# Two weight sums of the up projection formed by DRAM copies and adding transfers instead of on VectorE

## The chip, the cores and the metric

The kernel runs on one core of one Trainium2 chip. The metric is the device time of one execution in microseconds (us). A second execution was recorded by the hardware profiler; its page and trace are what this document reads. Engines are named as the profile names them: PE is TensorE (PEld its weight loads), DVE is VectorE, ACT is ScalarE, POOL is GpSimd, and SP is SyncE, which here only starts transfers.

## The reference

One layer of a decoder trunk, at 1024 positions and width 1024, all in float32:

```
h = rmsnorm(x)
[q | k | v | u | s | gate_a | gate_b] = h @ w_in
branch A: sliding-window attention (window 128, 8 query heads, 2 key heads)
branch B: u * (tril(W_s) @ rmsnorm(gelu(s)) + b), in chunks of 128 positions
x = x + (sigmoid(gate_a) * (A @ w_oa) + sigmoid(gate_b) * (B @ w_ob)) @ w_out
z = rmsnorm(x) @ w_up                       # 1024 x 5632
zc = causal depthwise convolution of z, width 3, plus bias
x = x + (silu(zc[gate half]) * zc[value half]) @ w_down
```

What the change touches is the product with w_up and the way the gates' and the down projection's inputs are combined for the same scheme.

## The kernel before

Matrices are held transposed: features on the 128 partitions, positions along the free dimension. Every float32 operand of a product is split in a high part (rounded to the form that PE takes) and a low part (the rest), and each product is three matmuls, high by high, high by low and low by high. ACT makes the high parts (`copy_hi`, L87), POOL or DVE the low ones by a subtraction (L988 for the weights of the gates and the up projection).

The gates, the up and the down projection are computed by a fast scheme on 2 x 2 blocks with seven products in place of eight (Strassen's scheme in Winograd's form). For the up projection, a *pair* is a gate tile and a value tile of 128 output features each. The four blocks of its weights are called A11, A12 (one tile's first and second half of the input features) and A21, A22 (the other tile's). Four sums of them are needed besides: S1 = A21 + A22, S2 = S1 - A11, S3 = A11 - A21 and S4 = A12 - S2. The right-hand blocks B11 to B22 have sums T1 to T4 of their own. `Blocks.prod` (L1028) runs one of the seven products, 12 matmuls of 512 columns; `Blocks.sums`, `fast_pair`, `gate_pair` and `v_end` add the products up on DVE. There are 22 pairs for the up projection and 8 for the gates.

S1 and S3 of the 22 up pairs are formed ahead of the up stage. `sums_load` loads A11 of a pair (256 KB) and A21 and A22 (512 KB) from w_up, `sums_step` makes the two sums on DVE in SBUF (L620, tile `ls`) and stores them to DRAM (tile `sum`, 512 KB). This is done 12 times among the gate pairs, twice in each from the third on, and 10 times among the branch products, where `branch` calls it. In the up stage `Left.load_q` and `Left.load_s3` load S1 and S3 back, with A22 from w_up; POOL makes S2 and S4 from them (`sum_s2`, `sum_s4`).

The stages in time: projection of keys and values (to about 50 us), attention (to 180 us), the normed values and the spatial products of branch B (`v_phase`, to about 220 us), the gates (`v_end`, `gate_pair`, to 381 us), the branch and output products (`run_jobs`, to 571 us), the up stage with the convolution (`fast_pair`, to 978 us) and the down projection.

Attention is one loop over n from 0 to 19 (L649 and on). Iteration n computes the scores of block n (`s_mm`, `s_mask`), the softmax of block n-1 (`s_exp`, whose last step is on POOL, L480), transposes and splits block n-2 (`p_split`, with four selects on POOL, L502 and L504) and multiplies block n-4 by the values (`pv_mm`). PE's waiting time is filled with pieces of other projections (`filler`). `weights(n)` splits the weight tile due in that iteration (the low part on POOL, L108 or L191) and starts the load of a later one on SP. The next stage's `v_phase` runs over s from 0 to 7: PE makes the halves of the value tile s, ACT the GELU, `v_rsqrt(s)` on DVE and POOL (L128, L129) the scale, `v_norm(s)` on DVE the normed values (L755), which frees the PSUM tile, and `v_split` the two parts for the spatial products (`sgu_mm`).

The order of work is written by hand: within a region marked `manual_schedule()` each engine issues its instructions in the order of the code. Attention is one such region and `v_phase` to the end another; where instructions of one region fall among those of the other on the same engine is left to the planner. Transfers that SP starts stand in SP's queue in the same way, and one that waits for a buffer holds up those behind it. POOL starts no transfer in this kernel.

Of the kernel before, what the change touches and what calls it, by code (L numbers as in the profile page):

```python
# [41 lines left out]
def body(ctx, tc, nc, a):  # L42
# [216 lines left out]

    st = {}  # L260

    def q_proj(n):
# [356 lines left out]
    def sub(eng, out, x, y, op=ALU.subtract):  # L619
        eng.tensor_tensor(out, x, y, op=op)  # L620
        return out

    def x_gain(r, ks):
        for k in ks:
            x = xr_raw[r][:, k, :]
            nc.scalar.activation(x, x, AF.Copy, scale=cp[:, 186 + 4 * r + k:187 + 4 * r + k])

    def x_sums(ks, first):
        for k in ks:
            x0 = xr_raw[0][:, k, :]  # L630
            if first:
                sub(nc.vector, x0[:, L], x0[:, H], x0[:, L])
            else:
                x1 = xr_raw[1][:, k, :]
                sub(nc.vector, x0[:, H], x1[:, H], x0[:, H])
# [6 lines left out]
    for n in range(20):  # L642
        if n < 16:
            s_mm(n)
            s_mask(n)
        if 0 <= n - 1 < 16:
            s_exp(n - 1)
        if n < 16:
            s_max(n)  # L649
        if 0 <= n - 4 < 16:  # L650
            pv_mm(n - 4)
        q_new = filler(n, 0)
        if 0 <= n - 2 < 16:
# [12 lines left out]
        if n == 17:  # L666
            x_gain(0, (0, 1))
        if n == 18:
            x_gain(0, (2, 3))
            x_sums((0, 1), True)  # L670
        if n == 19:
            x_sums((2, 3), True)
        for t, p in u_done:
            nc.vector.tensor_tensor(uT[:, t, :], p, rstd_b, op=ALU.mult)
        u_done.clear()
        if n + 2 < 16:
            q_trans(n + 2)
            q_split(n + 2)
        for q in [3] + q_new if n == 0 else q_new:
            q_norm(q)  # L680
# [105 lines left out]
    def v_phase():  # L786
# [32 lines left out]
    def v_end():  # L819
# [52 lines left out]
        nx.load_q()  # L872
        sums_load()
        q.prod(q.v1, "S2", "T2")
# [9 lines left out]
        nc.scalar.copy(x5, e)  # L884
        nc.vector.tensor_tensor(x7, x7, e, op=ALU.add)
        nc.vector.tensor_tensor(q.g1, x5, q.g1, op=ALU.add)
        nc.vector.tensor_tensor(q.v1, x7, q.v1, op=ALU.add)
        nc.vector.tensor_tensor(q.v0, q.u2, q.v0, op=ALU.add)
        q.scale(q.zv)
# [38 lines left out]
    class Left:  # L928
# [28 lines left out]
        def sum_s3(self):  # L957
            self.s3 = s3_pool.tile([128, 4, 128], F, tag="s3", name=nm("s3"))
            sub(nc.gpsimd, self.s3, self.p[:, 0:4], self.q[:, 0:4])

        def sum_f3(self):

            sub(nc.gpsimd, self.p[:, 0:4], self.q[:, 4:8], self.r[:, 0:4])

# [14 lines left out]
        def sum_s2(self):  # L979
            self.r = raw("lr")  # L980
            sub(nc.gpsimd, self.r[:, 0:4], self.q[:, 0:4], self.p[:, 0:4])

        def sum_s4(self):
            sub(nc.gpsimd, self.r[:, 4:8], self.p[:, 4:8], self.r[:, 0:4])

# [25 lines left out]
    class Blocks:  # L1011
# [38 lines left out]
    sums = {"load": 0, "make": 0}  # L1050

    def sums_load():

        i = sums["load"]
        if i < NPAIR:
            x = pools["ls"].tile([128, 3, 4, 128], F, tag="ls", name=nm("ls"), bufs=2)
            nc.sync.dma_start(x[:, 0], a["wup"][2 * i][:, 0:4])
            nc.sync.dma_start(x[:, 1:3], a["wup"][2 * i + 1].rearrange("p (b k) m -> p b k m", b=2))
            sums[i] = x
            sums["load"] += 1  # L1060

    def sums_step():

        i = sums["make"]
        if i < NPAIR:
# [6 lines left out]
            pools.setdefault("sum", {})[i] = t  # L1072
            sums["make"] += 1


# [26 lines left out]
    def gate_pair(c, prev):  # L1102
# [93 lines left out]
    def branch(n):  # L1196
        br, c = B_ORDER[n]

        def main(w):
# [66 lines left out]
    def out_tile(i):  # L1266
        d = D_ORDER[i]

        def main(w):
# [20 lines left out]
            if d < 4:  # L1290
                eng = nc.gpsimd if i < 6 else nc.vector
                right_split("B11", k, h[:, L], eng)
                sub(nc.vector, h[:, L], h[:, H], h[:, L])
                right_split("T1", k, h[:, L], eng)
            else:
                g = hs_[k]
                sub(nc.vector, g[:, H], h[:, H], g[:, H])
# [3 lines left out]
                t2 = sub(nc.vector, pools["raw2"][:, k, :], h[:, H], g[:, L])  # L1301
                sub(nc.vector, pools["raw4"][:, k, :], h[:, L], t2)
            if i == 0:
# [6 lines left out]
    def last_tile(w, ac):  # L1310
# [27 lines left out]
        g = hs_[k]  # L1338
        sub(nc.vector, g[:, H], h[:, H], g[:, H])
        right_split("B22", k, h[:, H], nc.vector)  # L1340
        right_split("T3", k, g[:, H], nc.vector)
        t2 = sub(nc.vector, pools["raw2"][:, k, :], h[:, H], g[:, L])
        sub(nc.vector, pools["raw4"][:, k, :], h[:, L], t2)

# [98 lines left out]
    def first_pair():  # L1443
# [31 lines left out]
        nx.split_s3()  # L1475
        nc.vector.tensor_tensor(x7, x7, u2, op=ALU.add)
        q.prod(q.g1, "S4", "B22", more=True)
# [9 lines left out]
        q.u2 = u2  # L1487
        nc.vector.tensor_tensor(q.v1, u2, x7, op=ALU.add)
        nc.vector.tensor_tensor(q.v0, u2, q.v0, op=ALU.add)

# [9 lines left out]
    def fast_pair(n, prev, q, hooks, rms=None):  # L1500
# [41 lines left out]
        if nx and not rms:  # L1542
            nx.split_p()
        nc.vector.tensor_tensor(x7, x7, q.g1, op=ALU.add)
        if rms:
# [235 lines left out]
def layout(x, mix_norm, w_in, q_norm, k_norm, sinks, sgu_norm, w_s, b_s,  # L1781
# [17 lines left out]
    up_order = np.stack([np.arange(NPAIR), np.arange(NPAIR) + NPAIR], 1).reshape(-1)  # L1799
    wup = tiles(w_up, 8)[up_order]  # L1800

    def pcol(v):
# [20 lines left out]
        "wout": tiles(w_out, 8),  # L1823
        "wup": wup,
        "wdown": c(w_down.reshape(NPAIR, 128, 1024)),
# [20 lines left out]
```

## Time and profile before

| | |
|---|---|
| Median of 3 runs | 1193.23 us (1193.14 to 1193.96) |
| Profiled execution | 1193.8 us, span 1192.1 us |
| Granted PE clock | 1.000 over the span |
| HBM read, written | 139.63 MB, 50.59 MB |
| DVE, sums of S1 and S3 (L620, tile ls) | 44 instructions, 269.7 to 468.0 us |
| POOL, rsqrt of the normed values (L129) | 8 instructions in 180 to 222 us, idle before them 21.9 us |
| PE waits that end on POOL or DVE in attention | 11 groups, the longest of them 1.3 us in all |

The span reaches from the first to the last instruction; the execution's own time has some microseconds around it. A row of instructions names the line of the kernel, the engine, the operation, and the tiles as output<-inputs with their shapes; behind `x` stands how many there are. Brackets at the end of a row give how long the engine stood idle before it and which instruction ended that. `SPq` rows are transfers that SP started: the length is that of the issue, not of the transfer.

### The profile page before, as it was taken

To read this page: it belongs to the slowest core of one execution; us is meant where nothing else is said; L and a number is where in the kernel's file an instruction comes from. 1 tells how busy PE (TensorE), PEld (TensorE's weight loads), DVE (VectorE), ACT (ScalarE), POOL (GpSimd) and SP (SyncE) were. 2 spreads that over 40 slices of the span, in tenths; PEclk is the share of its full clock that TensorE was granted. 3 is DMA by queue.
4 is the path that set the end of the run, shared out by engine and by line. 5 is a ranking of instruction groups with operands and counts; after the bars stand their busy time and mean duration, and the time that the engine had idled before them with its cause. 6 is when DMAs were issued, how large, how long until landed. Compare 5 with 4: busy or idle time off the path is not lost.

```text
span 1192.1 us, 15888 instructions
## 1 busy us (share of the span) xinstructions
PE 1180.0 (99%) x5890; PEld 1000.9 (84%) x5890; DVE 877.8 (74%) x1028; ACT 541.8 (45%) x832; POOL 567.4 (48%) x364
## 2 busy tenths in 40 slices
PE   8999999999999999999999999999999999999998
PEld 8989989988888888888888888888888888888887
DVE  7798975745638565668897788878788798865674
ACT  8555567644335222234544444444444445434331
POOL 2367685487768222343756575656657551000000
PEclk9999999999999999999999999999999999999999
DMA  7110133037786997342143342423333258966471
GB/s 272 35 54 19 54 136 130 5 130 260 245 315 212 347 327 278 125 165 100 54 142 108 104 143 98 148 91 124 108 131 124 89 209 290 373 230 194 151 233 67
DMA packets 79134, 191.27 MB, mean 160 GB/s; under 512 B 8913, under 2 KB 9169, under 8 KB 79057
## 3 DMA queue, kind: packets, MB, share of 16 engines
q1 hardware_dynamic: 79056, 190.26, 45.9%
q8 instruction: 46, 0.75, 0.3%
q14 instruction: 32, 0.25, 0.1%
HBM read 139.63 MB, written 50.59 MB: 160 GB/s over the span
## 4 chain that ended last, share of the span: by engine, by line
PE 89%; DVE 4%; POOL 1%; issue 1%; ACT 0%; POOLq 0%; DVEq 0%; ACTq 0%
PE pz L1028 48%; PE pd L1672 10%; PE pdy L1672 8%; PE px L93 2%; PE px L92 2%; PE po L93 2%; PE po L92 2%; PE po L91 2%; PE px L91 2%; PE pvs L91 1%; PE pvs L92 1%; PE pvs L93 1%; DVE ya L529 1%; PE pq L91 1%; PE pq L93 1%; PE pq L92 1%
## 5 line engine op out<-in xcount | busy, mean ns | idle before, releaser
L1028 PE MATMUL pz<-T,qh 128*128 128x512 f32 x472 | 145.6, 390 | 0.0
L988 POOL TENSOR_TENSOR pl<-lp,ph 128x1024 fp32r<-128x1024 f32 x30 | 72.5, 2418 | 83.5 <-ACT ph L87 83.3
L1028 PE MATMUL pz<-B,ph 128*128 128x512 f32 x352 | 109.1, 391 | 0.0
L1028 PEld LDWEIGHTS pz<-T,qh 128*128 128x128 f32 x472 | 88.5, 188 | 18.6 <-ACT u L879 0.3
L1028 PE MATMUL pz<-T,ql 128*128 128x512 f32 x236 | 91.8, 389 | 0.0
L108 POOL TENSOR_TENSOR wjl<-wj,wjh 128x512 fp32r<-128x512 f32 (+1 forms) x24 | 40.6, 1692 | 95.8 <-ACT wjh L87 95.8
L988 POOL TENSOR_TENSOR ql<-lq,qh 128x1024 fp32r<-128x1024 f32 x30 | 76.9, 2565 | 9.1 <-ACT qh L87 9.1
L1028 PEld LDWEIGHTS pz<-B,ph 128*128 128x128 f32 x352 | 65.3, 188 | 15.0 <-ACT x L1519 1.8
L1044 DVE TENSOR_TENSOR pz<-pz,rstd_b 128x1024 f32<-128x1024 f32 x60 | 73.9, 1232 | 4.2 <-ACT rstd_b L141 2.1
L988 POOL TENSOR_TENSOR s3l<-s,s3h 128x512 fp32r<-128x512 f32 x29 | 39.8, 1373 | 69.7 <-ACT s3h L87 69.7
L1028 PE MATMUL pz<-T,s3h 128*128 128x512 f32 x232 | 71.4, 389 | 0.0
L1028 PE MATMUL pz<-B,pl 128*128 128x512 f32 x176 | 68.6, 390 | 0.0
L1672 PE MATMUL pd<-bl,ah 128*128 128x512 f32 x176 | 68.5, 389 | 0.0
L1672 PE MATMUL pd<-bh,ah 128*128 128x512 f32 x176 | 68.5, 389 | 0.0
L1672 PE MATMUL pd<-bh,al 128*128 128x512 f32 x176 | 68.5, 389 | 0.0
L1028 PE MATMUL pz<-T,AX 128*128 128x512 f32 x264 | 63.4, 389 | 0.0
L1028 PE MATMUL pz<-B,AX 128*128 128x512 f32 x264 | 63.4, 389 | 0.0
L1028 PEld LDWEIGHTS pz<-T,AX 128*128 128x128 f32 x264 | 49.6, 188 | 10.3
L1028 PEld LDWEIGHTS pz<-B,AX 128*128 128x128 f32 x264 | 49.6, 188 | 10.3
L1378 DVE SCALAR_TENSOR_TENSOR tg<-pz,cp,tg 128x1023 f32<-128x1023 f32 (+1 forms) x44 | 56.2, 1278 | 0.8
L1378 DVE SCALAR_TENSOR_TENSOR tv<-pz,cp,tv 128x1023 f32<-128x1023 f32 (+1 forms) x44 | 56.2, 1277 | 0.8
L988 POOL TENSOR_TENSOR AX<-lr,AX 128x1024 fp32r<-128x1024 f32 x22 | 53.7, 2440 | 5.1 <-ACT AX L87 5.1
(342 smaller groups left out, 3511.8 us busy)
## 6 DMA issues: line engine op xcount, KB each, us to landing
ls<-wup SPq DMA_DIRECT2D x22, 512.0 KB, 5.3
sum<-ls SPq DMA_DIRECT2D x22, 512.0 KB, 5.3
lp<-wup SPq DMA_DIRECT2D x22, 512.0 KB, 3.6
ra<-wdown SPq DMA_DIRECT2D x44, 256.0 KB, 4.6
b<-T SPq DMA_DIRECT2D x44, 256.0 KB, 3.8
B<-tv SPq DMA_DIRECT2D x33, 256.0 KB, 2.0
T<-tt SPq DMA_DIRECT2D x33, 256.0 KB, 2.0
b<-B SPq DMA_DIRECT2D x33, 256.0 KB, 3.1
```

The lines of the kernel that those rows point to most:

```text
L91: nc.tensor.matmul(out, wh, mh, start=first, stop=False, **kw)
L92: nc.tensor.matmul(out, wh, ml, start=False, stop=False, **kw)
L93: nc.tensor.matmul(out, wl, mh, start=False, stop=last, **kw)
L108: nc.gpsimd.tensor_tensor(l[:, :nk, :], r[:, :nk, :], h[:, :nk, :].bitcast(F), op=ALU.subtract)
L529: nc.vector.tensor_tensor(ya[r, 2 * half:2 * half + 2, b * 128:(b + 1) * 128], p[r, g], o[r], op=ALU.add)
L988: nc.gpsimd.tensor_tensor(l, r, h.bitcast(F), op=ALU.subtract)
L1028: nc.tensor.matmul(o, p[:, k, :], y[:, q, k, :], start=not more and k == 0 and j == 0, stop=k == 3 and j == 2, skip_group_check=True)
L1044: nc.vector.tensor_tensor(z, z, rstd_b, op=ALU.mult)
L1378: nc.vector.scalar_tensor_tensor(t[:, j:], p[:, 0:1024 - j], cw[:, ci, 2 - j:3 - j], t[:, j:], op0=ALU.mult, op1=ALU.add)
L1672: nc.tensor.matmul(o[d], p[:, k - k0, m], q[:, k - k0, :], start=new and k == 0 and j == 0, stop=k == HK - 1 and j == 2, skip_group_check= ...
```

## The change

S1 and S3 of the 22 up pairs are no longer formed on DVE. In iterations 0 to 10 of attention SP starts two copies each, DRAM to DRAM, of a pair's (A11, A21) into a 512 KB tensor (`sum_copy`). Then POOL starts an adding transfer for each (`sum_add`), which adds (A21, A22) onto it, so that the tensor holds A11 + A21 and A21 + A22. Adds 0 to 7 stand at the end of the odd iterations 1 to 15, behind `p_split` and `weights`; adds 8 to 21 stand two each in the steps s = 0 to 6 of `v_phase`, between `v_gelu(s)` and `v_rsqrt(s)`. Each add waits for its copy to have landed.

An adding transfer can't subtract, so S3 is A11 + A21 now. The signs of the other sums are turned to match, on the weights' side (S2 = S1 + A11, S4 = A12 + S2), on the right-hand side (T1 to T4), and where the products are added up. Some sums change places with differences; `neg_sum` forms -x - y on DVE in one scalar_tensor_tensor.

The up weights are stored per pair as A11, A21, A22, A12, so that the copy and the add each read two neighbouring blocks; the load of A11 and A12 takes two blocks of 2 KB a partition. `sums_load` and `sums_step` are gone with their loads, sums and stores, and the 12 KB a partition of their tiles in the pool `ls`.

The diff, with repeated sign changes left out:

```diff
+    sums = {}
+
+    def rows4k(t):
+        return t.rearrange("(p b) m -> p (b m)", b=2)
+
+    def sum_copy(i):
+        sums[i] = dr.tile([256, 512], F, tag=f"sum{i}", name=f"sum{i}")
+        nc.sync.dma_start(rows4k(sums[i]), rows4k(a["wup"][i, 0:2].rearrange("b p m -> (b p) m")))
+
+    def sum_add(i):
+        nc.gpsimd.dma_start(rows4k(sums[i]), rows4k(a["wup"][i, 1:3].rearrange("b p m -> (b p) m")), accum_op=ALU.add, max_dma_last_dim=4096)
...
+    def neg_sum(out, x, y):
+        nc.vector.scalar_tensor_tensor(out, x, -1.0, y, op0=ALU.mult, op1=ALU.subtract)
+        return out
...
-                sub(nc.vector, x0[:, L], x0[:, H], x0[:, L])
+                sub(nc.vector, x0[:, L], x0[:, L], x0[:, H])
...
-                sub(nc.vector, x1[:, H], x1[:, H], x0[:, L])
-                sub(nc.vector, x1[:, L], x1[:, L], x1[:, H])
+                neg_sum(x1[:, H], x0[:, L], x1[:, H])
+                sub(nc.vector, x1[:, L], x1[:, L], x1[:, H], ALU.add)
...
         weights(n)
+        if n < 11:
+            sum_copy(2 * n)
+            sum_copy(2 * n + 1)
+        if n in (1, 3, 5, 7, 9, 11, 13, 15):
+            sum_add(n // 2)
...
             v_gelu(s)
+            for i in range(8 + 2 * s, min(10 + 2 * s, NPAIR)):
+                sum_add(i)
...
         nx.load_q()
-        sums_load()
...
-            nc.sync.dma_start(self.q[:, 0:4], pools["sum"][self.i][:, 1])
-            nc.sync.dma_start(self.q[:, 4:8], self.sq[:, 4:8])
+            nc.sync.dma_start(self.q[:, 0:4], sums[self.i][128:256])
+            nc.sync.dma_start(self.q[:, 4:8], self.sq)
...
-            nc.sync.dma_start(self.s3, pools["sum"][self.i][:, 0])
+            nc.sync.dma_start(self.s3, sums[self.i][0:128])
...
-            sub(nc.gpsimd, self.r[:, 0:4], self.q[:, 0:4], self.p[:, 0:4])
+            sub(nc.gpsimd, self.r[:, 0:4], self.q[:, 0:4], self.p[:, 0:4], ALU.add)
...
-            nc.vector.tensor_tensor(self.v0, self.u2, m4, op=ALU.add)
-            nc.vector.tensor_tensor(self.v1, x7, self.v1, op=ALU.add)
+            sub(nc.vector, self.v0, m4, self.u2)
+            sub(nc.vector, self.v1, x7, self.v1)
...
-    def sums_step():
-
-        i = sums["make"]
-        if i < NPAIR:
-            sums_load()
-            x = sums.pop(i)
-            sub(nc.vector, x[:, 0], x[:, 0], x[:, 1])
-            sub(nc.vector, x[:, 1], x[:, 1], x[:, 2], ALU.add)
-            t = pools["dr"].tile([128, 2, 4, 128], F, tag=f"sum{i}", name=f"sum{i}")
-            nc.sync.dma_start(t, x[:, 0:2])
...
-        if c > 1:
-            sums_step()
         q.prod(q.v0, "S3", "T3")
...
-        nc.vector.tensor_tensor(x7, x7, q.g1, op=ALU.add)
+        sub(nc.vector, x7, x7, q.g1)
         if nx:
             nx.sums_r()
-        if c > 1:
-            sums_step()
...
-            if n % 2 == 0 or n in (5, 9):
-                sums_step()
...
-    lefts = [Left(a["wup"][2 * i], a["wup"][2 * i + 1], i) for i in U_ORDER]
+    lefts = [Left(a["wup"][i, 0::3].rearrange("b p m -> p b m"), a["wup"][i, 2], i) for i in U_ORDER]
...
-    wup = tiles(w_up, 8)[up_order]
+    wup = tiles(w_up, 8)[up_order].reshape(NPAIR, 2, 128, 2, 512)
+    wup = np.stack([wup[:, 0, :, 0], wup[:, 1, :, 0], wup[:, 1, :, 1], wup[:, 0, :, 1]], axis=1)
```

More of the change, by code (lines that the diff above doesn't have):

```diff
@@ L884, in v_end @@
         nc.scalar.copy(x5, e)
-        nc.vector.tensor_tensor(x7, x7, e, op=ALU.add)
+        sub(nc.vector, x7, x7, e)
         nc.vector.tensor_tensor(q.g1, x5, q.g1, op=ALU.add)
-        nc.vector.tensor_tensor(q.v1, x7, q.v1, op=ALU.add)
-        nc.vector.tensor_tensor(q.v0, q.u2, q.v0, op=ALU.add)
+        sub(nc.vector, q.v1, x7, q.v1)
+        sub(nc.vector, q.v0, q.v0, q.u2)
         q.scale(q.zv)
@@ L958, in sum_s3 @@
             self.s3 = s3_pool.tile([128, 4, 128], F, tag="s3", name=nm("s3"))
-            sub(nc.gpsimd, self.s3, self.p[:, 0:4], self.q[:, 0:4])
+            sub(nc.gpsimd, self.s3, self.p[:, 0:4], self.q[:, 0:4], ALU.add)
         def sum_f3(self):
-            sub(nc.gpsimd, self.p[:, 0:4], self.q[:, 4:8], self.r[:, 0:4])
+            sub(nc.gpsimd, self.p[:, 0:4], self.r[:, 0:4], self.q[:, 4:8])
         def first_s3(self):
@@ L980, in sum_s2 @@
             self.r = raw("lr")
-            sub(nc.gpsimd, self.r[:, 0:4], self.q[:, 0:4], self.p[:, 0:4])
+            sub(nc.gpsimd, self.r[:, 0:4], self.q[:, 0:4], self.p[:, 0:4], ALU.add)
         def sum_s4(self):
-            sub(nc.gpsimd, self.r[:, 4:8], self.p[:, 4:8], self.r[:, 0:4])
+            sub(nc.gpsimd, self.r[:, 4:8], self.p[:, 4:8], self.r[:, 0:4], ALU.add)
         def split(self, names, r, h, l):
@@ L1048, in last_sum @@
             self.scale(self.zg)
-    sums = {"load": 0, "make": 0}
-    def sums_load():
-        i = sums["load"]
-        if i < NPAIR:
[L1056 to L1060, printed above, removed]
-    def sums_step():
-        i = sums["make"]
-        if i < NPAIR:
-            sums_load()
-            x = sums.pop(i)
-            sub(nc.vector, x[:, 0], x[:, 0], x[:, 1])
-            sub(nc.vector, x[:, 1], x[:, 1], x[:, 2], ALU.add)
-            t = pools["dr"].tile([128, 2, 4, 128], F, tag=f"sum{i}", name=f"sum{i}")
-            nc.sync.dma_start(t, x[:, 0:2])
-            pools.setdefault("sum", {})[i] = t
-            sums["make"] += 1
     jobs.clear()
@@ L1292, in main @@
                 right_split("B11", k, h[:, L], eng)
-                sub(nc.vector, h[:, L], h[:, H], h[:, L])
+                sub(nc.vector, h[:, L], h[:, L], h[:, H])
                 right_split("T1", k, h[:, L], eng)
@@ L1296, in main @@
                 g = hs_[k]
-                sub(nc.vector, g[:, H], h[:, H], g[:, H])
+                sub(nc.vector, g[:, H], g[:, H], h[:, H])
                 right_split("B21", k, h[:, L], nc.vector)
@@ L1300, in main @@
                 right_split("T3", k, g[:, H], nc.vector)
-                t2 = sub(nc.vector, pools["raw2"][:, k, :], h[:, H], g[:, L])
-                sub(nc.vector, pools["raw4"][:, k, :], h[:, L], t2)
+                t2 = neg_sum(pools["raw2"][:, k, :], g[:, L], h[:, H])
+                sub(nc.vector, pools["raw4"][:, k, :], h[:, L], t2, ALU.add)
             if i == 0:
@@ L1338, in last_tile @@
         g = hs_[k]
-        sub(nc.vector, g[:, H], h[:, H], g[:, H])
+        sub(nc.vector, g[:, H], g[:, H], h[:, H])
         right_split("B22", k, h[:, H], nc.vector)
         right_split("T3", k, g[:, H], nc.vector)
-        t2 = sub(nc.vector, pools["raw2"][:, k, :], h[:, H], g[:, L])
-        sub(nc.vector, pools["raw4"][:, k, :], h[:, L], t2)
+        t2 = neg_sum(pools["raw2"][:, k, :], g[:, L], h[:, H])
+        sub(nc.vector, pools["raw4"][:, k, :], h[:, L], t2, ALU.add)
     late = {}
@@ L1475, in first_pair @@
         nx.split_s3()
-        nc.vector.tensor_tensor(x7, x7, u2, op=ALU.add)
+        sub(nc.vector, x7, x7, u2)
         q.prod(q.g1, "S4", "B22", more=True)
@@ L1487, in first_pair @@
         q.u2 = u2
-        nc.vector.tensor_tensor(q.v1, u2, x7, op=ALU.add)
-        nc.vector.tensor_tensor(q.v0, u2, q.v0, op=ALU.add)
+        sub(nc.vector, q.v1, x7, u2)
+        sub(nc.vector, q.v0, q.v0, u2)
         def rms():
@@ L1543, in fast_pair @@
             nx.split_p()
-        nc.vector.tensor_tensor(x7, x7, q.g1, op=ALU.add)
+        sub(nc.vector, x7, x7, q.g1)
         if rms:
@@ L1823, in layout @@
         "wout": tiles(w_out, 8),
-        "wup": wup,
+        "wup": c(wup),
         "wdown": c(w_down.reshape(NPAIR, 128, 1024)),
```

2 lines of the change are left out of this document (1 added, 1 removed).

## The prediction

> **What bounds the kernel now.** I read the page's first part, then the table of busy time by stage, the list of who waited for whom cut to TensorE (PE), and the chain of waits in order of time.
>
> ```profile
> PE 1180.0 (99%) x5890; PEld 1000.9 (84%) x5890; DVE 877.8 (74%) x1028; ACT 541.8 (45%) x832; POOL 567.4 (48%) x364
> ...
> 0.00:52.00 52.00, 47.31 (x365) 45.75 (x366) 37.10 (x71) 33.86 (x63) 15.06 (x17) 1.00 0.50 176
> 52.00:180.00 128.00, 124.74 (x874) 113.93 (x874) 110.91 (x236) 78.61 (x250) 89.73 (x99) 1.00 0.18 63
> 180.00:245.00 65.00, 65.00 (x485) 61.82 (x484) 42.98 (x61) 46.32 (x68) 32.58 (x23) 1.00 0.26 94
> 245.00:381.00 136.00, 136.00 (x602) 112.58 (x601) 75.65 (x79) 58.82 (x72) 105.18 (x60) 1.00 0.67 230
> 381.00:580.00 199.00, 199.00 (x894) 165.34 (x893) 135.33 (x126) 60.28 (x78) 75.62 (x43) 1.00 0.57 207
> 580.00:978.00 398.00, 398.00 (x1756) 328.37 (x1755) 329.38 (x315) 181.79 (x212) 241.65 (x123) 1.00 0.36 122
> 978.00:1192.00 214.00, 209.91 (x926) 173.13 (x924) 146.41 (x143) 82.16 (x92) 7.55 (x4) 1.00 0.64 220
> ```
>
> In a stage row, the second column is its length, then come the busy times of PE, weight load, DVE, ACT and POOL, the granted clock, and the DMA engines' busy share. From 180 to 978 us PE has no idle time at all. What is idle lies in the head (52.00 - 47.31 = 4.7 us), in attention (128.00 - 124.74 = 3.3 us) and at the end (4.1 us), 12 us together. A full row could still hide a slower pace, so I compare it in the chain of waits:
>
> ```profile
> 244.64 136.26 PE pz L1028 x600
> ...
> 580.39 397.86 PE pz L1028 x1752
> 978.24 29.92 PE pd L1672 x132
> ```
>
> 136.26/600, 397.86/1752 and 29.92/132 are all 0.227 us a matmul, with DMA shares of 0.67, 0.36 and 0.64 and DVE from half to four fifths busy. So neither the DMA traffic nor DVE's load in the gates and the up stage sets the pace there. Only attention and the stage up to 222 us can answer to this change.
>
> **What it removes.** The forming of S1 and S3 in SBUF:
>
> ```profile
> L620 DVE TENSOR_TENSOR ls<-ls 128x512 f32<-128x512 f32 x44 | 44.5, 1010 | 9.4 <-DMA ls<-wup 8.6
> ...
> ls<-wup SPq DMA_DIRECT2D x22, 512.0 KB, 5.3
> sum<-ls SPq DMA_DIRECT2D x22, 512.0 KB, 5.3
> ```
>
> That is 44.5 us of DVE, and 22 x (256 + 512 + 512 KB) = 29 MB of transfers with their SP issues, all after 237 us and most of it between 270 and 470 us, where PE is full. SP's next weight loads no longer stand behind a store that waits for DVE. All of this is off the path that sets the end: worth **0**, and at most the 1 us by which the two long PE pieces miss the best pace (136.26 + 397.86 less 2352 x 0.2267).
>
> **What only changes form.** A sum in place of a difference on DVE or POOL is the same instruction. The two-step form of neg_sum (a scalar_tensor_tensor) is priced by two DVE rows of 128x512 quoted below: 0.75 against 0.68 us, so +0.07 us each, 4 in the stage before the gates and 8 in the output stage; the first make 0.3 us on a DVE that has gaps there, the others lie under a full PE: 0, and 0.3 without that cover. The up stage's load of A11 and A12 comes as two 2 KB pieces a partition instead of one of 4 KB, at a DMA share of 0.36 and with PE never waiting: 0.
>
> **What it adds on SP and the DMA engines.** 22 copies of 512 KB from DRAM to DRAM go on SP's queue in iterations 0 to 10, two each, behind that iteration's weight load.
>
> ```profile
> q1 hardware_dynamic: 79056, 190.26, 45.9%
> ...
> 61.72 6.04 SPq L97 DMA_DIRECT2D u<-wu  x2
> ...
> 186.39 1.76 SPq L616 DMA_DIRECT2D xa<-xw  x4
> 191.97 2.18 ACT L626 ACTIVATE xa<-xa,cp 128x1024 f32<-128x1024 f32 x2
> ...
> 171.30 0.33 SPq L97 DMA_DIRECT2D lp<-wgb  x1
> ...
> 65.00 2.41 POOL L191 TENSOR_TENSOR wq<-q,wq 128x1024 fp32r<-128x1024 f32 x1
> ```
>
> 190.26 MB took 45.9% of 1192 us, so the engines move 348 MB a ms and 512 KB take 1.5 us. A copy both reads and writes: 1.5 us if these overlap, 3.0 if not. An adding transfer reads two streams and writes one: 1.5 to 4.5 us. Together 66 to 165 us. Between 62 and 222 us the engines stand some 80% free, about 125 us. I take the middle, about 110 us: it fits. Copy 0 is issued behind the load at 61.72, and its add comes behind POOL's split that ends at 67.4; at a landing time of 5.3 us like that of the 512 KB rows it is just there. The loads queued behind the copies are needed iterations later. The four residual rows issued at 186.39 share the engines with adds 8 and 9; ACT needs the first at 192 us, and I let a microsecond there lie under the larger POOL delay below.
>
> **What it adds on POOL.** 22 adding transfers are started by POOL, in its order: adds 0 to 7 at the end of the odd iterations, 8 to 21 two in each step s = 0 to 6 before the GELU'd values are normed, ahead of that step's rsqrt (L129). POOL has no transfer in this trace, so its hold A for one is unknown. Bounds: SP's issue of one transfer (0.33 us) below, POOL's split of a 128x1024 tile (2.43 us) above. I take **A = 1.0 us**, by POOL's nearest row with a fixed cost and next to no data, 1.01 us on 128x4.
>
> ```profile
> 105.92 1.01 POOL L282 TENSOR_TENSOR qss<-qss,mh 128x4 f32<-128x4 f32 x1 [1.79 <-DVE qss L281]
> 109.47 0.63 POOL L453 TENSOR_SCALAR_AFFINE_SELECT c<-c 128x512 f32<-128x512 f32 x1
> ...
> 110.14 0.70 DVE sm L464
> ...
> 113.59 0.39 PE pq L91
> ...
> 173.82 2.43 POOL L191 TENSOR_TENSOR wvB<-z,wvB 128x1024 fp32r<-128x1024 f32 x1
> 178.20 0.97 POOL L504 TENSOR_SCALAR_AFFINE_SELECT cl<-cl 128x512 fp32r<-128x512 f32 x1
> ...
> 179.22 1.09 PE pv L517 x7
> ```
>
> *Attention.* Most adds fall into POOL's gaps. Two don't. Add 3 stands right before the mask of iteration 8 (109.47), and the chain goes from that mask through DVE's maximum (110.14), which DVE stood waiting for, to PE at 113.59: +1.0 us. Add 7 stands in a stretch without gaps, which ends with the select at 178.20 and releases PE at 179.22: +1.0 us. Adds 8 and 9 may also be drawn in there (the order between the two regions is the planner's); I leave them in the 5.77 us gap of the next fence, and count them in the range, +2.
>
> *The stage behind it*, by POOL's order and what waits for it:
>
> ```profile
> 187.77 0.55 POOL L129 TENSOR_TENSOR vss<-vss,mh 128x1 f32<-128x1 f32 x1 [5.77 <-DVE vss L128]
> ...
> 191.76 1.30 POOL L620 TENSOR_TENSOR lq<-lq 128x512 f32<-128x512 f32 x1
> 193.01 0.58 POOL L129 TENSOR_TENSOR vss<-vss,mh 128x1 f32<-128x1 f32 x1
> 193.54 1.31 POOL L620 TENSOR_TENSOR lr<-lq,lp 128x512 f32<-128x512 f32 x1
> 196.19 0.54 POOL L129 TENSOR_TENSOR vss<-vss,mh 128x1 f32<-128x1 f32 x1 [1.34 <-DVE vss L128]
> ...
> 201.84 0.54 POOL L129 TENSOR_TENSOR vss<-vss,mh 128x1 f32<-128x1 f32 x1 [2.14 <-DVE vss L128]
> ...
> 196.76 0.75 DVE L755 SCALAR_TENSOR_TENSOR vg<-pvs,vss,sg_b 128x512 f32<-128x512 f32 x1 [0.65 <-POOL vss L129]
> ...
> 199.94 0.28 PE L91 MATMUL pvs<-wv,x 128*128 128x256 f32 x1
> ...
> 212.72 0.68 DVE L759 TENSOR_TENSOR vsl<-vg,vsh 128x512 fp32r<-128x512 f32 x1
> ...
> L91 PE MATMUL pm<-wgh,vsh x32: 276/281/284, 214.1 to 235.9; 128*128 128x256 f32 x32
> ```
>
> Adds 10 and 11 go before the rsqrt at 193.01, 12 and 13 before that at 196.19, and only the 1.34 us gap lies between: the third rsqrt starts 4A - 1.3 = 2.7 us late. The fourth starts 6A - 3.3 = 2.7 us late (gaps 1.34 and 2.14). DVE waits for each in its norm (L755), with the splits behind it, so DVE runs 2.7 us late until its gaps return it. PE needs the third norm's buffer at 199.94, 2.4 us after it is free now, and takes 0.3 us there; but the first spatial product at 214.1 needs the split that ends at 212.72 + 0.68 = 213.4, so of the 2.7 us 0.7 are slack and **2.0 us** are a PE stall (the 0.3 is part of it).
>
> **Sum:** 1.0 + 1.0 + 2.0 = +4.0 us at A = 1.0. As a function, 2A + max(0, 4A - 2.0, 6A - 4.0): 0.7 us at A = 0.33, 1.3 at 0.55, 6.8 to 7.2 at 1.4, 12 at 2.0. The profiled run took 1193.8 us, 1.7 around its span of 1192.1; it would go to 1197.8. The median before is 1193.23, 0.6 lower, so I forecast **1197.2 us**.
>
> The Trainium skill weighs in on A: "SBUF — State Buffer", section "A bandwidth-pool intuition that's wrong (but worth ruling out)", gives a POOL-started transfer about 0.62 us alone and 3.1 us beside a DVE copy that holds the port they share. As an estimate from that page the sum would be 1.7 us by the first and 21 us by the second; DVE's rows in these stages are no such copies, which speaks for the first, and no run here shows either yet.
>
> **Rivals.**
> *Hidden.* POOL is 48% busy; if it lets a transfer go as fast as SP does (0.33 us), the rsqrts are not late (4 x 0.33 = 1.3 us, just the gap) and 0.7 us stays: **1193.9 us**, not slower in what can be measured. For it: POOL's gaps before most adds; against it: even POOL's smallest row, 128x1, takes 0.54.
> *POOL held.* Adds 8 to 21 come between 182 and 215 us, and take the engines up to 14 x 4.5 = 63 us. If POOL can't run far ahead of them, or DVE holds it up while it starts one, a hold of 2.0 us gives 12 us: **1205 us**. That these engines hold each other up is in two rows of one DVE operation, the longer begun beside a POOL split:
>
> ```profile
> 160.25 2.18 DVE L465 SCALAR_TENSOR_TENSOR sm<-sm,nsink 128x4 f32<-128x4 f32 x1
> ...
> 110.86 0.27 DVE L465 SCALAR_TENSOR_TENSOR sm<-sm,nsink 128x4 f32<-128x4 f32 x1
> ```
>
> By the Trainium skill, "SBUF — State Buffer", section "Who interferes with whom", the two share a port pair as an exclusive lock; the trace agrees for compute (2.18 against 0.27 us) and has no transfer on POOL.
> *Faster.* The same two rows read the other way: the hold of 2.18 us stands on the chain, and add 6, some five us ahead of it, shifts POOL against DVE. If this hold and another like it fall away, 3.8 us go, and with exposures of 0.7 us the time is **1190 us**. More would need PE's 12 us of idle time, which the removed work doesn't touch.
>
> **How the numbers follow.** Forecast 0.50 (its own range 1194.5 to 1200.5, from A = 0.55 to 1.4), hidden 0.28, POOL held 0.14, faster 0.08. The range takes in the hidden case and the 12 us: 1192.0 to 1205.5. No change can be told within 0.2%, 2.4 us, which A = 0.73 reaches (1.5 + 0.9). Slower: nine tenths of the forecast and all of POOL held, 0.59, less a little for slack that I may have missed: 0.57. Faster by over 0.2%: 0.06. Between: 0.37.
>
> **What would show it.** Right: POOL's transfers at about 1 us each; the third and fourth rsqrt some 2.7 us behind TensorE's schedule; a PE wait before the first spatial product and at the iteration 8 mask; the up stage as long as before. Wrong: rows of POOL's transfers far from 1 us, PE waits on the residual rows' loads, or a changed pace of 0.227 us a matmul after 245 us.

## The result, and the profile after

The changed kernel takes 1206.32 us (median of 4 runs, 1205.29 to 1207.77) against 1193.18 us before in the same comparison: a ratio of 1.0111, 95% interval 1.0093 to 1.0128, 13.1 us slower. The direction was forecast, the size was not: +4.0 us were predicted. The profiled execution is the fastest of the four, 1205.29 us with a span of 1203.6 us, so its trace has 11.5 us to explain (1203.6 - 1192.1).

First the page of the changed kernel: the span, the engines' busy times, the two DMA queues that the copies and adds use (packets, MB, share of 16 engines), and the two kinds of transfer with their KB and median time from issue to landing.

```profile
span 1203.6 us, 15806 instructions
...
PE 1182.9 (98%) x5890; PEld 1001.2 (83%) x5890; DVE 839.4 (70%) x984; ACT 543.1 (45%) x832; POOL 577.8 (48%) x386
...
q1 hardware_dynamic: 73072, 172.96, 42.1%
q0 software_dynamic: 3168, 11.54, 5.3%
...
sum<-wup SPq DMA_DIRECT2D x22, 512.0 KB, 9.1
sum<-wup POOLq DMA_DIRECT2D x22, 512.0 KB, 8.0
```

DVE lost 38 us of work (877.8 to 839.4) and PE does the same matmuls, yet the span grew. The busy time by stage, in the columns explained with the prediction, says where:

```profile
52.00:180.00 128.00, 121.51 (x829) 110.50 (x828) 112.20 (x231) 74.47 (x244) 90.94 (x102) 0.99 0.61 178
180.00:245.00 65.00, 59.74 (x469) 56.52 (x468) 37.55 (x58) 45.23 (x67) 41.01 (x39) 1.00 0.82 186
245.00:381.00 136.00, 136.00 (x612) 112.77 (x611) 48.16 (x56) 57.67 (x72) 101.10 (x60) 1.00 0.37 128
381.00:580.00 199.00, 199.00 (x879) 164.77 (x878) 119.50 (x101) 64.23 (x82) 69.82 (x40) 1.00 0.41 143
580.00:978.00 398.00, 398.00 (x1768) 328.41 (x1767) 328.57 (x316) 180.06 (x211) 249.95 (x127) 1.00 0.35 117
```

PE's idle time in attention went from 3.3 to 6.5 us and in the stage behind it from 0 to 5.3; after 245 us PE is full, as before. The granted clock of attention is 0.99 and not 1.00, which will matter. The chain of waits (start, length, what) has the long pieces of the later stages at the same length as before:

```profile
255.81 136.22 PE pz L1049 x600
...
591.52 398.27 PE pz L1049 x1752
```

The first of them started at 244.64 before: 11.2 of the 11.5 us are lost by then. To split them, follow two of POOL's own steps, the softmax multiply of each block (tile c<-c,sm) and the first rsqrt of the stage behind (tile vss, 187.77 to 188.32 before). First and last multiply of 16, before:

```profile
62.09 1.04 POOL L480 TENSOR_TENSOR c<-c,sm 128x512 f32<-128x512 f32 x1 [0.40 <-ACT qs L87]
...
167.87 1.04 POOL L480 TENSOR_TENSOR c<-c,sm 128x512 f32<-128x512 f32 x1
```

and after, with add 7 and add 8 (L271) and the first rsqrt:

```profile
61.70 1.04 POOL L491 TENSOR_TENSOR c<-c,sm 128x512 f32<-128x512 f32 x1 [0.41 <-DVE sm L490]
...
173.32 0.85 POOL L271 DMA_DIRECT2D sum<-wup  x1
173.92 1.32 POOL L491 TENSOR_TENSOR c<-c,sm 128x512 f32<-128x512 f32 x1
...
179.04 1.13 POOL L271 DMA_DIRECT2D sum<-wup  x1
...
195.63 0.57 POOL L129 TENSOR_TENSOR vss<-vss,mh 128x1 f32<-128x1 f32 x1 [6.01 <-DVE vss L128]
```

The markers on POOL are compared by their ends (start plus length). Behind an add a row is recorded as starting before the one ahead of it has ended, here at 173.92 with the add ending at 174.17, and the engines that use the result wait for its end: DVE's norm behind the rsqrt that ends at 207.83 starts at 207.86.

| Stretch | Marker, after less before | Lost in the stretch |
|---|---|---|
| to the end of the first multiply | -0.39 | -0.4 |
| attention, to the end of the 16th multiply | 6.33 | 6.7 |
| tail of attention, to the end of the first rsqrt | 7.88 | 1.6 |
| stage behind, to the start of the first long piece of the gates | 11.17 | 3.3 |
| all the rest, to the end of the span | 11.5 | 0.3 |

### The profile page after: what moved, and what is told of

It reads as the page before. It is cut to its first block, busy times and chain, and to the rows that moved or that the text cites. A ratio compares the mean times of both kernels' runs of the same rounds, so it can differ in the third digit from the quotient of the medians.

```text
span 1203.6 us, 15806 instructions
## 1 busy us (share of the span) xinstructions
PE 1182.9 (98%) x5890; PEld 1001.2 (83%) x5890; DVE 839.4 (70%) x984; ACT 543.1 (45%) x832; POOL 577.8 (48%) x386
## 3 DMA queue, kind: packets, MB, share of 16 engines
q0 software_dynamic: 3168, 11.54, 5.3%
## 4 chain that ended last, share of the span: by engine, by line
PE 84%; DVE 6%; POOL 3%; issue 2%; ACT 1%; ACTq 0%; POOLq 0%; DVEq 0%
PE pz L1049 47%; PE pd L1661 10%; PE pdy L1661 7%; PE px L92 2%; PE px L91 2%; PE po L92 2%; PE po L91 2%; PE po L93 2%; PE px L93 2%; DVE sm L476 1%; POOL sum L271 1%; DVE ya L540 1%; DVE qs L314 1%; PE pq L91 1%; DVE c L468 1%
## 5 line engine op out<-in xcount | busy, mean ns | idle before, releaser
L1049 PEld LDWEIGHTS pz<-T,AX 128*128 128x128 f32 x264 | 49.5, 188 | 10.3
L1049 PEld LDWEIGHTS pz<-B,AX 128*128 128x128 f32 x264 | 49.5, 188 | 10.3
```

The lines of the kernel that those rows point to most:

```text
L1049: nc.tensor.matmul(o, p[:, k, :], y[:, q, k, :], start=not more and k == 0 and j == 0, stop=k == 3 and j == 2, skip_group_check=True)
```

## The experiments

The theories: the transfers that POOL starts cost the time (by holding POOL, by holding DVE through POOL, or by waiting for room), against the rivals that the copies' traffic, the removed work or the new signs matter. Each run was compared with the kernel before on the same chip (medians of before 1193.1 to 1194.1 us).

**Copies without adds.** The 22 adds are left out, all else is the changed kernel.

```diff
-        if n in (1, 3, 5, 7, 9, 11, 13, 15):
-            sum_add(n // 2)
...
-            for i in range(8 + 2 * s, min(10 + 2 * s, NPAIR)):
-                sum_add(i)
```

> All 22 copies stay, the 22 adding transfers are left out (S1 and S3 then hold A21 and A11 alone). Theory 1, POOL's time for starting the adds and its place in POOL's order costs the 13 us: nothing of it is left, 1193 to 1194.5 us. Theory 2, the DRAM traffic delays other transfers: the copies are a good third of it, so 1197 us or more, with PE waits that end on transfers or on engines behind them.

1193.98 us, ratio 0.9997 (0.9988 to 1.0007). Attention's PE time is 124.69 us (124.74 before), and 180 to 245 us is full again. So the removed DVE work and its 29 MB, the signs and the copies come to nothing together, and all 13 us come with the adds.

**The adds by halves.** In the first run only adds 0 to 7 are left, in the second only adds 8 to 21; the other adds of each are left out, by one of the two hunks above.

> Adds 0 to 7 stay, adds 8 to 21 of the next stage are left out (those pairs' S1 and S3 are not summed). Theory 1: in the changed kernel's trace POOL's last softmax step stands 6.0 us later than before, so 1193.2 + 6 = 1199 us, with the drop of the granted clock at 86 to 90 us as before. Theory 2: two thirds of the traffic, about 1201 us.

> Adds 8 to 21 stay, adds 0 to 7 are left out (those pairs' S1 and S3 are not summed). Theory 1: adds 8 and 9 in the tail of attention cost 2 us and the next stage some 3 to 5, 1198 to 1200 us, and the two parts together make the 13 us. My prediction had 2 us for this part alone. Theory 2: the same size, but PE waits in the stage end on transfers.

1201.22 us, 1.0059 (1.0042 to 1.0075): +7.1 us. 1199.95 us, 1.0046 (1.0031 to 1.0061): +5.8 us. The sum of 12.9 fits the 13.1 well, but partly by luck, because each contains a stretch of low granted clock (below) of which the whole change has only one.

**What an add does in attention.** Add 1 is the clearest. POOL before, with the multiply of block 3 and the select behind it:

```profile
79.83 1.04 POOL L480 TENSOR_TENSOR c<-c,sm 128x512 f32<-128x512 f32 x1 [0.68 <-DVE sm L479]
81.16 0.64 POOL L502 TENSOR_SCALAR_AFFINE_SELECT eh<-ch 128x512 fp32r<-128x512 f32 x1 [0.29 <-ACT ch L87]
```

DVE before, right behind its maximum:

```profile
80.27 0.62 DVE L465 SCALAR_TENSOR_TENSOR sm<-sm,nsink 128x4 f32<-128x4 f32 x1
```

POOL after, add 1 between the select ahead of it and the same two:

```profile
78.80 0.64 POOL L515 TENSOR_SCALAR_AFFINE_SELECT cl<-cl 128x512 fp32r<-128x512 f32 x1
79.38 0.89 POOL L271 DMA_DIRECT2D sum<-wup  x1
80.02 1.33 POOL L491 TENSOR_TENSOR c<-c,sm 128x512 f32<-128x512 f32 x1
81.02 0.92 POOL L513 TENSOR_SCALAR_AFFINE_SELECT eh<-ch 128x512 fp32r<-128x512 f32 x1
```

DVE after:

```profile
80.26 1.71 DVE L476 SCALAR_TENSOR_TENSOR sm<-sm,nsink 128x4 f32<-128x4 f32 x1
```

The add starts in POOL's idle gap of 0.68 us, as predicted, and the multiply ends only 0.48 us later than before (81.35 against 80.87). But look at the small operation of DVE. Before, it ends at 80.89, when POOL's multiply ends: it is held until then. After, the select is recorded as starting at 81.02, 0.33 us before the multiply ends, and DVE's operation ends at 81.97, when the *select* ends (81.94). All that DVE does next is 1.08 us late, down to the piece that PE's scores wait for (uT): they start at 84.94 us, before at 83.86. The Trainium skill, "SBUF — State Buffer", section "Who interferes with whom", has the rule: a DVE instruction with two inputs in SBUF contends with a GpSimd one that reads SBUF, and the later one is blocked for the whole instruction. The rows agree, and add that behind an add it can stay blocked over two POOL instructions. Add 6 does the same (1.67 us from 160.08).

It is not a pause on POOL that lets DVE in. In the kernel before, the operation that the prediction shows at 160.25 us ends at 162.43, with POOL's split, although the multiply follows the split at once:

```profile
159.99 2.42 POOL L191 TENSOR_TENSOR wv<-v,wv 128x1024 fp32r<-128x1024 f32 x1
162.37 1.04 POOL L480 TENSOR_TENSOR c<-c,sm 128x512 f32<-128x512 f32 x1
```

There the two rows overlap by 0.04 us, behind add 1 by 0.33. That this overlap is what keeps DVE out is the likely reading; no run varied it.

The hold is one part of add 1's price. The other is in the 2 us windows behind it (same columns):

```profile
82.00:84.00 2.00, 1.07 (x6) 0.66 (x4) 1.95 (x5) 0.79 (x3) 0.20 (x1) 1.00 1.11 328
84.00:86.00 2.00, 1.06 (x9) 1.09 (x10) 1.64 (x3) 1.71 (x9) 1.65 (x3) 1.00 0.74 197
86.00:88.00 2.00, 2.00 (x14) 2.00 (x13) 1.77 (x5) 0.41 (x2) 0.00 (x0) 0.59 0.95 160
88.00:90.00 2.00, 2.00 (x12) 2.00 (x12) 1.92 (x5) 0.33 (x1) 1.04 (x1) 0.56 0.48 94
```

PE idles 1.87 of 4 us, and then its granted clock is 0.59 and 0.56 for 4 us: 4 x (1 - 0.575) = 1.7 us lost at a full PE. The Trainium skill, "TensorE: Matmul & The Clock Gate", section "What's actually happening", has a clock that goes to half after an idle window of some 3.4 us, the windows running free of the program. As an estimate from that page, half the clock for 3.4 us loses 1.7 us, which agrees in size; an idle window is not what the trace shows, PE being busy for over half of the 4 us.

**One add less.** Adds 0 to 7 without add 1, which with adds 8 to 21 is left out.

```diff
-        if n in (1, 3, 5, 7, 9, 11, 13, 15):
+        if n in (1, 5, 7, 9, 11, 13, 15):
             sum_add(n // 2)
```

> As adds_in_attention, with add 1 (iteration 3) left out too. In the trace that add is followed by a DVE hold of 1.1 us, a PE wait of 2.0 us and a granted clock of 0.6 at 86 to 90 us. If this add is their cause: no drop of the clock, and 2.5 to 3 us less, 1198 to 1199 us. If each add costs the same: 0.9 us less, 1200.3 us.

1197.87 us, 1.0036 (1.0022 to 1.005): 4.3 us over before where all eight adds made 7.1, so one of them takes 2.8. The low clock at 86 us is gone with it, and so is a part of the hold. The low clock is not tied to that place, though: in the two runs on the adds' size below, add 1 stays and PE idles 2.4 and 1.8 us between 82 and 86 us, but the clock stays at 1.00 there and falls at 186 to 190 us, to 0.71 and 0.65 and then 0.50. Each trace with adds in attention or behind it has one such stretch, except this run's and the next one's. The rows of DVE's small operation from 52 to 187 us (count, busy us, mean ns, idle before), in the kernel before:

```profile
L465 DVE SCALAR_TENSOR_TENSOR sm<-sm,nsink 128x4 f32<-128x4 f32 x16 | 10.4, 652 | 0.5
```

and in the changed kernel:

```profile
L476 DVE SCALAR_TENSOR_TENSOR sm<-sm,nsink 128x4 f32<-128x4 f32 x16 | 14.6, 913 | 0.5
```

In the changed kernel this one operation takes 4.2 us more in all. Without add 1 the same row stands at 13.2 us, a mean of 826 ns.

**The same eight adds in other places.** Adds 0 to 7 stand right behind POOL's multiply instead of ahead of the next one, in iterations 2, 3 and 5 to 10 instead of the odd ones to 15; adds 8 to 21 are left out.

```diff
+ADD_AT = (2, 3, 5, 6, 7, 8, 9, 10)
...
             s_exp(n - 1)
+        if n in ADD_AT:
+            sum_add(ADD_AT.index(n))
...
-        if n in (1, 3, 5, 7, 9, 11, 13, 15):
-            sum_add(n // 2)
```

> Adds 0 to 7 in attention as in the run adds_in_attention (and 8 to 21 left out), but each right behind the softmax's last step on POOL, in the iterations 2, 3, 5, 6, 7, 8, 9 and 10, where POOL then waits 1.8 us for DVE, instead of at the end of an iteration, ahead of that step. If the loss comes from the place in POOL's order (the step starts late, and DVE's small operation on two SBUF inputs is held behind it): nearly all of the 7 us is gone, 1194 to 1196 us, and the mean of that DVE operation falls from 0.91 back to about 0.65 us. If starting a transfer on POOL costs wherever it is: 1199 to 1202 us.

1194.58 us, 1.0007 (0.9997 to 1.0017): nothing that can be measured, where the same eight adds cost 7.1 us. The add is as long as ever, as POOL's rows show behind the multiply of block 2:

```profile
72.81 1.04 POOL L492 TENSOR_TENSOR c<-c,sm 128x512 f32<-128x512 f32 x1 [0.39 <-DVE sm L491]
73.80 0.88 POOL L272 DMA_DIRECT2D sum<-wup  x1
```

and DVE's operation, the group of 52 to 187 us in the same run, is back at its time of before:

```profile
L477 DVE SCALAR_TENSOR_TENSOR sm<-sm,nsink 128x4 f32<-128x4 f32 x16 | 10.8, 676 | 0.5
```

So POOL's own time for a start is not the price in attention; its place is.

**The adds' size.** Two runs of the changed kernel: each add over an eighth of the bytes (64 KB instead of 512, the rest of each sum is left out), and each add whole but in rows of 8 KB instead of 4.

```diff
-        nc.gpsimd.dma_start(rows4k(sums[i]), rows4k(a["wup"][i, 1:3].rearrange("b p m -> (b p) m")), accum_op=ALU.add, max_dma_last_dim=4096)
+        nc.gpsimd.dma_start(rows4k(sums[i][0:32]), rows4k(a["wup"][i, 1:3].rearrange("b p m -> (b p) m")[0:32]), accum_op=ALU.add, max_dma_last_dim=4096)
```

```diff
-        nc.gpsimd.dma_start(rows4k(sums[i]), rows4k(a["wup"][i, 1:3].rearrange("b p m -> (b p) m")), accum_op=ALU.add, max_dma_last_dim=4096)
+        def rows8k(t):
+            return t.rearrange("(p b) m -> p (b m)", b=4)
+
+        nc.gpsimd.dma_start(rows8k(sums[i]), rows8k(a["wup"][i, 1:3].rearrange("b p m -> (b p) m")), accum_op=ALU.add, max_dma_last_dim=8192)
```

> All 22 adds are started where they were, each with 64 KB in place of 512 KB (the rest of S1 and S3 is not summed). If the start on POOL alone costs it: 1203 to 1206 us, as with the whole adds. If it is POOL waiting for earlier adds to move (or the traffic): attention as in the changed kernel, but the idle stretches of POOL before adds in the next stage (1 to 2.7 us) vanish, and 2 to 4 us come back: 1202 to 1204 us. Theory 2: about 1195 us plus what the copies cost.

> The changed kernel with each add in 64 rows of 8 KB in place of 128 rows of 4 KB, so half the descriptors for the same bytes. If POOL waits in the stage behind attention for room for descriptors: the idle stretches before its adds (0.5 to 2.7 us) vanish as with the short adds, 1.5 to 2 us less than the changed kernel, 1204 to 1205 us. If it waits for bytes to be moved: unchanged, 1206 us.

1204.46 us, 1.0084 (1.0069 to 1.0099), and 1203.05 us, 1.008 (1.0062 to 1.0099). Most of the cost, 10.3 of 13.1 us, stays when seven eighths of the adds' traffic are gone, so the DMA engines are not what binds there. What both take away is seen in POOL's rows of the stage behind attention. The changed kernel, adds 12 and 13 with the third rsqrt, and the fourth rsqrt:

```profile
203.82 1.49 POOL L271 DMA_DIRECT2D sum<-wup  x1
206.42 0.81 POOL L271 DMA_DIRECT2D sum<-wup  x1 [1.12 <-issue]
206.97 0.86 POOL L129 TENSOR_TENSOR vss<-vss,mh 128x1 f32<-128x1 f32 x1
...
213.07 0.56 POOL L129 TENSOR_TENSOR vss<-vss,mh 128x1 f32<-128x1 f32 x1 [0.65 <-DVE vss L128]
```

With rows of 8 KB, from the first rsqrt:

```profile
195.33 0.57 POOL L129 TENSOR_TENSOR vss<-vss,mh 128x1 f32<-128x1 f32 x1 [7.63 <-DVE vss L128]
...
203.48 2.19 POOL L274 DMA_DIRECT2D sum<-wup  x2
204.79 1.48 POOL L129 TENSOR_TENSOR vss<-vss,mh 128x1 f32<-128x1 f32 x1
```

"Issue" is time in which POOL waited for nothing that the profile shows: 1.12, 0.47, 2.70, 1.04 and 1.50 us ahead of five adds, 6.8 us in all. None is left in the two runs, one of which moves every byte. They differ from the changed kernel in packets, 3168 for the 22 adds against 1760 with rows of 8 KB and 704 with short adds. So a POOL that starts adds close together probably waits for room for its packets. The size of that room was not varied; that it is full is argued from the packets, and a POOL still busy with the packets of earlier adds would look the same. The price is the same in both runs: from the end of the first rsqrt to the first long piece of the gates they lose 1.6 us, the changed kernel 3.3.

**The adds among the branch and output products.** All 22 whole adds, one at the end of each of the 16 branch jobs and one ahead of each of the first six output tiles; the two hunks of their old places go.

```diff
                 m_split(c)
+            sum_add(n)
...
+            if i < 6:
+                sum_add(16 + i)
             p = PS("px")
```

> The whole sums, with the copies as in the change and all 22 adds in the stage of the branch and output products, where POOL is idle for 62% and PE full: one behind each of the 16 branch products, six ahead of output tiles 0 to 5. If the place decides: as before the change, 1193 to 1195 us. If adds cost wherever they are: 1200 us or more. Faster than before by more than 1 us: only if the work taken off DVE had been worth something, which the run copies_only speaks against.

1193.5 us, 0.9997 (0.9988 to 1.0007). The change as a whole costs nothing there, and gains nothing. From 381 to 580 us the DMA engines are busier, 0.71 against 0.41 with copies alone, which is 60 us for 22 adds or 2.7 us each, and PE stays full:

```profile
381.00:580.00 199.00, 199.00 (x895) 165.26 (x894) 120.01 (x104) 59.81 (x77) 90.91 (x65) 1.00 0.71 199
```

**VectorE's order turned.** If DVE's hold behind the reciprocal is the mechanism, the loss should go when the hold does. `s_exp` is cut in two: the denominator, its reciprocal and POOL's multiply of block n-1 now come behind the maximum of block n and its two small operations, so that POOL isn't multiplying when DVE reads. First in the changed kernel, then, the same edit, in the kernel before.

```diff
         nc.scalar.activation(es, es, AF.Exp)
+
+    def s_norm(n):
+        c, sm = st[("c", n)]
+        den, es = sm[:, 1, :], sm[:, 2, :]
         nc.vector.tensor_tensor(den, den, es, op=ALU.add)
...
             s_max(n)
+        if 0 <= n - 1 < 16:
+            s_norm(n - 1)
```

> The changed kernel with one order turned on DVE: in each iteration of attention the maximum of block n and its two small operations come before the denominator and reciprocal of block n-1, so that DVE's small operation on two SBUF inputs no longer stands right behind the reciprocal that releases POOL's softmax step. Adds and POOL's own order are unchanged. If attention's loss comes over DVE being held beside that step (its group grew from 10.4 to 14.6 us): the group falls to some 5 us, and 2 to 4 us of attention's 6.5 come back, 1202 to 1204 us; what is lost behind attention stays. If it comes from POOL's results being late alone: 1206 us or more, as these are released a microsecond later still.

> The same turn of DVE's order in the kernel before the change. DVE is held there too, about 0.4 us an iteration, but PE is idle for only 3.3 us in attention: between no change and 1.5 us less, 1192 to 1193.5 us. Above 1194 us if the later release of POOL's step is the greater loss.

The changed kernel: 1197.76 us, 1.0042 (1.0027 to 1.0057), with DVE's operation at 6.0 us in all; that is more than was expected to come back. The kernel before: **1189.89 us, 0.997 (0.9958 to 0.9981)**, faster than both kernels and better than was expected of it. DVE's operation there, the same group of rows:

```profile
L465 DVE SCALAR_TENSOR_TENSOR sm<-sm,nsink 128x4 f32<-128x4 f32 x16 | 5.7, 358 | 0.5
```

and attention as a whole (124.74 us of PE before):

```profile
52.00:180.00 128.00, 126.98 (x906) 117.28 (x906) 105.38 (x239) 80.67 (x253) 91.54 (x99) 1.00 0.19 65
```

The pair also shows what the adds cost in attention in this order: from the end of the first multiply to that of the sixteenth the changed kernel loses 1.3 us against the kernel before in the same order, where it lost 6.7 in the old one. That is not the hold alone: the multiply is released later in this order, which leaves POOL room for an add (behind add 1 it starts after 2.05 us, in the changed kernel after 0.64), and the low clock moves out of attention. What stays of the 7.9 us is the tail (3.5, with the granted clock down to 0.74 and 0.50 from 178 to 182 us) and the stage behind (3.0).

**Both together.** The adds among the products and the turned order, whole sums.

> The whole sums, their adds among the products, and VectorE's order turned (the next block's maximum ahead of the finished block's denominator). If the removed VectorE work is worth nothing even where the adds cost nothing, this is before_max_first again: 1189 to 1191 us, a ratio of 0.996 to 0.998. If the removed work shows once the softmax order no longer covers it, it is below 1189 us. If the adds cost something that adds_among_products had hidden behind the old order's waits, it is above 1191.5 us.

1189.94 us, 0.9973 (0.9964 to 0.9982), the time of the turned order alone within 0.05 us. Even where no add costs anything, the 44.5 us taken from DVE are worth nothing.

## Why the prediction was right or wrong

**Right: what was removed is worth nothing.** The step "All of this is off the path that sets the end: worth 0" holds in three runs: copies without adds, the adds among the products, and the last pair, 1189.94 against 1189.89 us. The long pieces of PE kept their pace (136.22 us for 600 matmuls, 136.26 before).

**Right: signs and copies.** Zero in the first run; the rows of neg_sum are 0.69 us long, not 0.75. A copy lands 9.1 us after its issue, not the 5.3 assumed, but POOL waits for none: no add has a wait on a DMA. The engine time of an add, estimated at 1.5 to 4.5 us, is 2.9 (5.3% of 16 engines over 1203.6 us, by 22). The residual rows' loads hold up nothing.

**Nearly right: POOL's hold A = 1.0.** The rows of the transfers are 0.81 to 1.49 us long, median 0.88. POOL's next instruction is recorded as starting 0.6 us after the add's start (79.38 to 80.02, 173.32 to 173.92), but its row is then 0.3 us longer, and what waits for POOL waits for the end. At add 1 the end of the select ahead (79.44) and the end of the multiply behind (81.35) lie 1.91 us apart, of which the multiply alone takes 1.04: a hold of 0.87. By the formula of the prediction, 2A + max(0, 4A - 2.0, 6A - 4.0), that gives +3.2 us. (The gaps of 1.34 and 2.14 us make 3.5 and not 3.3, so the fourth rsqrt's 2.7 should have been 2.5; and at A = 1.4 the formula gives 7.2, not 6.8 to 7.2. Little rests on either.) The rival of a held POOL, whose 1205 us were nearest to the result, needed 2.0 us and is wrong in that; only its clause that POOL can't run far ahead of the DMA engines turned out to be there, as the waits for room. *Hidden* needed 0.33 us. *Faster* needed the hold of 2.18 us to fall away; it is still 2.17 in the changed kernel.

**The step that failed: "Most adds fall into POOL's gaps. Two don't."** The two exposures that were named are there, at their place and at the price of a hold of 0.9: over add 3, by way of the mask of iteration 8, the multiply's end goes from 3.29 to 4.26 us late (blocks 6 and 8), over add 7 from 5.47 to 6.33 (blocks 14 and 15). Together 1.8 us of attention's 6.7. The other 4.9 come from adds that were counted at nothing. Most of that, 3.0, comes behind adds 1 and 2: the multiply of block 2 is 0.28 us late, that of block 4 1.26 (the hold of DVE behind add 1) and that of block 6 3.29 (the clock, and at most 0.7 for add 2, which is what that stretch loses without add 1). Adds 0, 4 and 6 make the other 1.9. The working asked what POOL loses by a later start, and not who is held while POOL runs on, and it had no term for the granted clock. The evidence on the hold was in the prediction, in its last fence, and was misread: both rows are held by POOL, the long one until the split ends (162.41), the short one until the multiply begun at 110.07 ends (111.11); the same operation takes 0.16 us when nothing holds it (61.92 us in the kernel before with the order turned). It was read as a chance to gain.

**The tail.** Adds 8 and 9 were drawn in between the last selects, as the prediction allowed in its range at +2; it is +1.6. The chain of waits of the changed kernel runs through POOL there:

```profile
179.62 0.42 POOL cl L515
...
180.22 2.95 POOL wvB L191
183.17 0.81 POOL sum L271
183.97 0.93 POOL eh L513
...
186.60 0.64 POOL cl L515
187.24 0.04 issue
187.29 1.08 PE pv L528 x7
```

Everything between 180.22 and 187.24 is POOL, add 9 in the middle. PE waits for these selects.

**The stage behind: the hold right, the wait for room missing, the stall elsewhere.** The third rsqrt was to be 2.7 us late against the first; by their ends it is 3.2 (207.83 - 196.20 = 11.63, before 196.73 - 188.32 = 8.41), the fourth 3.4 instead of 2.7. With A = 0.87 the hold alone gives 4A - 1.34 = 2.1, and the run with 8 KB rows, which has no wait for room, shows 2.0 (206.27 - 195.90 = 10.37). The rest is the wait for room, 1.12 us ahead of add 13. PE's stall was put at 2.0 us, in front of the first spatial product. PE's waits from 168 to 245 us in the changed kernel (us in total, times, longest):

```profile
PE pv L528 <- POOL cl L515: 1.8, 3, 0.9
PE pm L91 <- ACT pm L924: 1.5, 1, 1.5
PE pv L528 <- POOL ch L515: 1.3, 1, 1.3
PE pvs L91 <- DVE vg L775: 1.2, 1, 1.2
```

The two that belong to this stage make 2.7: 1.2 at the third norm's buffer, where 0.3 were expected, none in front of the first spatial product, and 1.5 later at a buffer of the spatial products. With 8 KB rows the first of the two is gone and the second stays.

In sum: the prediction's 4.0 us stand against 11.5 in the trace. Attention is mis-sized by 4.7 (6.7 for 2.0), the tail by 1.6 (nothing was put in the sum for it) and the stage behind by 1.3 (3.3 for 2.0); the first and the last row of the table make the difference. The median of the four executions lies another 1.0 us above the profiled one. The upper end of the range, 1205.5 us, was made from longer holds alone and fell 0.8 us short of the median.

## What to carry to other kernels

The price of an instruction put on an engine that is off the critical path isn't its length but who is kept out while that engine runs on: look for the small operation of another engine that waits for that engine's current instruction to end, and put the new work where it doesn't move that end or close what follows it. The same eight adds cost 7.1 us ahead of POOL's multiply, and nothing that could be measured right behind it. And where a row shows an operation at several times its shortest length, turn that order first: here it gave 3.5 us to the kernel before, more than 44.5 us of DVE work taken off a part that TensorE fills.

## What the runs showed of the hardware

A transfer that POOL starts in attention has a row of 0.85 to 1.0 us. POOL's next instruction is recorded as beginning after 0.6, but some 0.3 us longer (the multiply 1.33 instead of 1.04), so that its result comes 0.9 us later than without the add. A DVE operation of 128x4 with its inputs in SBUF took 0.16 us alone, 0.6 when begun beside POOL's multiply, and 1.67 to 1.71 where an add made the next POOL row overlap the multiply. Started close together, such transfers kept POOL waiting up to 2.7 us each at 144 packets apiece (3168 for 22), and not at 80 (1760).

PE's granted clock fell to 0.50 to 0.74, by windows of 2 us, for some 4 us behind idle time of 1.6 to 2.2 us within 4, in attention or in its tail. What sets it off stays open: at 184 to 188 us the changed kernel's PE idled 2.2 of 4 us, with short adds it idled 2.4 of 4 us from 82 to 86, and both times the clock stayed at 1.00 for the next 4 us.
